# Moving the low parts of U's blocks from VectorE to GpSimd in a decoder layer with expert retrieval

## The chip, the cores and the metric

The kernel runs on one core of one Trainium2 chip. The metric is the device time of one execution in microseconds; a kernel's figure is the median of its runs. One further execution was recorded by the hardware profiler, and all rows below are from it.

## What is computed

The layer has two halves. The first mixes tokens (512 tokens of 1024 features, two groups of eight attention heads, one output projection). The second is a retrieval over 16384 experts of one neuron each, and the change lies in it:

```python
def chunk(hc):                                   # 128 tokens
    q = (hc @ w_q).reshape(-1, PEER_HEADS, PEER_KEY_DIM)
    s1 = jnp.einsum('chd,nd->chn', q[..., :half], k1)
    s2 = jnp.einsum('chd,nd->chn', q[..., half:], k2)
    v1, i1 = lax.top_k(s1, PEER_TOPK)            # 16 of 128
    v2, i2 = lax.top_k(s2, PEER_TOPK)
    cand_s = v1[..., :, None] + v2[..., None, :]
    cand_i = i1[..., :, None] * N_KEYS + i2[..., None, :]
    best_s, best_pos = lax.top_k(cand_s, PEER_TOPK)
    expert = jnp.take_along_axis(cand_i, best_pos, axis=-1)
    g = jax.nn.softmax(best_s, axis=-1)
    act = jax.nn.gelu(jnp.einsum('cd,chkd->chk', hc, u[expert]), approximate=False)
    return jnp.einsum('chk,chkd->cd', g * act, v[expert])
```

Each token picks 128 experts (8 heads of 16). `u` and `v` have 16384 rows of 1024 numbers in float32.

## The kernel before

The tokens are four tiles of 128. For tiles 0 to 2 the kernel does not gather: it multiplies their tokens with all 16384 rows of `u`, in 128 blocks of 128 experts, applies GELU, multiplies by a gate matrix that is zero where a token did not pick an expert, and multiplies the result with all rows of `v`. Tile 3 is done by gathering (`gather_ops`, lines 906 to 923): 128 indirect DMAs of rows of `u` and 128 of `v`, issued by GpSimd, each followed by one VectorE instruction.

Products keep float32 accuracy by splitting: an operand becomes a high part (rounded by ScalarE to the matmul's type `fp32r`) and a low part (operand minus high part), and three products are added: high with high, high with low, low with high (`mm3`, lines 146 to 149).

`u_block` (lines 864 to 881) does one block of U. The 512 KB of rows arrive over SyncE's DMA queue in a tile `raw` (line 866, two buffers); ScalarE makes `hi` (line 870), VectorE or GpSimd makes `lo` (line 871; GpSimd for the blocks in `UPOOL`), two buffers each; TensorE does 8 times the three products of `mm3` with the tokens `h2` (lines 873 and 874; lines 147, 148, 149 in the trace); ScalarE evacuates with GELU into `a` (line 877). Load and split are given a higher priority than what stands around them (`UPRI`), so that the scheduler lays them down early.

Blocks 0 to 55 (`NAHEAD` = `NACT` + `NSPILL`) are done ahead of V, beside the making of the gates. Their results stay in SBUF (`NACT` = 40 buffers) but for the first `NSPILL` = 16, which are written to DRAM (line 879) and read back later (line 988). Beside these blocks run, per token tile:

- `route` (lines 703 to 737): scores on TensorE (line 710), then top-k by VectorE's MAX8, MATCH_REPLACE8 and FIND_INDEX8 (lines 717 to 721, 733 to 737); GpSimd casts the indices (line 723).
- `choose` and `spread` (lines 739 to 804): many VectorE instructions on 128x64 to 128x2048 elements, some on ScalarE (line 765).
- per group of 16 tokens, twice, `hot` (lines 806 to 817): three one-hot tiles `oh` by VectorE, in two buffers each; then `gates` (lines 821 to 837): 16 products of 128x128 (line 831), two times, ScalarE's evacuation (line 834), and a store `g_d` (line 837).

The order written out is the loop at lines 938 to 951: token tiles 0, 1, 2, each of eight groups, two U blocks behind each group (`GPAT`), with `route` and `choose` of the coming tile placed by `WHEN`; four blocks stand ahead of it and two behind the first `choose` (`U0`), and line 952 does what is left of the 56. The framework's scheduler turns this into one fixed list of instructions per engine, by priority and by when it reckons operands to be ready; each engine then works off its list in order, waiting at an instruction until its operands are there. Gathers may so be laid ahead of their place in the text.

The second loop (lines 1032 to 1052) runs over V's 128 blocks: `v_load` loads and splits V's rows and the gated `a` (ScalarE and VectorE), `v_mm` does 18 products of 512 columns (line 1004). From block `NSPILL` on, one U block (56 to 127) follows each V block (line 1039). The gathers of tile 3 are dealt out over the blocks by `RATE` (line 1029), with one rate for b < `NSPILL`, one for b < `NK - NACT` and one for the rest. V can start only when all gates are stored, since each of its blocks reads a slice of all of them (line 970).

Of the kernel before, what the change touches and what calls it, by code (L numbers as in the profile page):

```python
# [9 lines left out]
F32 = mybir.dt.float32  # L10
# [11 lines left out]
P = 128  # L22
D = 1024
KC = D // P
# [12 lines left out]
GSCALE = 32768.0  # L37
ND = NT - 1
DT = ND * P
NACT = 40  # L40
NSPILL = 16
NAHEAD = NACT + NSPILL
VB = 2
WHEN = ((0, 2), (3, 5))
# [9 lines left out]
XAT = (0, 1)  # L54
UPRI = 1000
PACE = 1.02
UPOOL = tuple(range(0, 56, 4))
LAST = 4
VRB = 3
ARB = 3  # L60
# [14 lines left out]
def hybrid_layer(ctx: ExitStack, tc, x, pos, wada, wada_n, cols, w_small, w_in_a, w_in_b, wuk, wuv,  # L75
                 w_out, w_pq, keys, ut, un, pv, gfin, cst, out):
    nc = tc.nc

    def opened(stack, name, **kw):
        if "space" not in kw:  # L80
            kw["reuse_waits"] = "tile"
        return stack.enter_context(tc.tile_pool(name=name, bufs=1, **kw))
# [8 lines left out]
    def one(name, tag="tp"):  # L91
        return ps.tile([P, 512], F32, tag=tag, name=name, bufs=BANKS[tag])

    x1_d = [dram.tile([P, D], F32, name=f"x1_d{j}") for j in range(NT)]
    a_d = [dram.tile([P, DT], F32, name=f"a_d{b}") for b in range(NSPILL)]
    g_d = [dram.tile([P, P // 16, NK, 16], F32, name=f"g_d{j}") for j in range(ND)]
# [49 lines left out]
    def mm3(o, ahi, alo, bhi, blo, start, stop, **kw):  # L146
        nc.tensor.matmul(o, ahi, bhi, start=start, stop=False, **kw)  # L147
        nc.tensor.matmul(o, ahi, blo, start=False, stop=False, **kw)  # L148
        nc.tensor.matmul(o, alo, bhi, start=False, stop=stop, **kw)  # L149
# [24 lines left out]
    def row_back(s, pl, tag, bufs):  # L174
        t = pl.tile([P, D], F32, tag=tag, name=f"gate{s}", bufs=bufs)
        nc.sync.dma_start(t, row_d[s].to_broadcast([P, D]))
        return t
# [95 lines left out]
    for half in range(2):  # L273
# [3 lines left out]
        for k in range(KC):  # L277
            a, b = eff[0][:, k:k + 1], mods[0][:, k:k + 1]
# [301 lines left out]
    for step in SEQ_A.split():  # L580
        what, i = step[0], int(step[1])
# [77 lines left out]
    h2 = []  # L659
# [181 lines left out]
    for n in range(2):  # L841
        his, los = wchunks(wo, [w_pq[n]], 512, f"pq{n}", 16, 2)
        for j in range(NT):
            o = one(f"p_q{n}_{j}", "pl")
# [14 lines left out]
    up = opened(ctx, "up", side="right")  # L859
# [3 lines left out]

    def u_block(b, psum):
        with tc.high_priority(offset=UPRI):
            raw = up.tile([P, KC, P], F32, tag="raw", name=f"u{b}", bufs=2)
            nc.sync.dma_start(raw.rearrange("p k e -> p (k e)"), ut[b])
            hi = up.tile([P, KC, P], F32R, tag="hi", name=f"uhi{b}", bufs=2)
            lo = up.tile([P, KC, P], F32R, tag="lo", name=f"ulo{b}", bufs=2)
            nc.scalar.activation(hi, raw, AF.Copy)  # L870
            (nc.gpsimd if b in UPOOL else nc.vector).tensor_tensor(lo, raw, hi.bitcast(F32), op=ALU.subtract)  # L871
        o = psum(f"p_u{b}")[:, :DT]
        for k in range(KC):
            mm3(o, hi[:, k], lo[:, k], h2[0][:, k], h2[1][:, k], k == 0, k == KC - 1)
        spilt = b < NSPILL
        a = up.tile([P, DT], F32, tag="as" if spilt else "a", name=f"a{b}", bufs=2 if spilt else NACT)
        nc.scalar.activation(a, o, AF.Gelu)  # L877
        if spilt:
            nc.sync.dma_start(a_d[b], a)
            a = a_d[b]  # L880
        acts.append(a)
# [3 lines left out]
    def u_ahead(n):  # L885
        for _ in range(n):
            if nu[0] < NAHEAD:
                u_block(nu[0], lambda n: one(n, ("pj", "po", "ix")[nu[0] % 3]))
                nu[0] += 1
# [76 lines left out]
    def v_load(b):  # L966
        if b % 8 == 0:
            gt = vp.tile([P, ND, P // 16, 8, 16], F32, tag="gt", name=f"gt{b}", bufs=2)
            for j in range(ND):
                nc.sync.dma_start(gt[:, j].rearrange("p g i t -> p g (i t)"),  # L970
                                  g_d[j][:, :, b:b + 8, :].rearrange("p g i t -> p g (i t)"))
            gts[0] = gt
        raw = vp.tile([P, D], F32, tag="raw", name=f"v{b}", bufs=VRB)
        nc.sync.dma_start(raw, pv[b * P:(b + 1) * P, :])
        late = b >= NK - LAST + VB
        if late:
            hi = up.tile([P, D], F32R, tag="hi", name=f"vhi{b}", bufs=2)
            lo = up.tile([P, D], F32R, tag="lo", name=f"vlo{b}", bufs=2)
        else:
            hi = vp.tile([P, D], F32R, tag="vhi", name=f"vhi{b}", bufs=VB)  # L980
            lo = vp.tile([P, D], F32R, tag="vlo", name=f"vlo{b}", bufs=VB)
        nc.scalar.activation(hi, raw, AF.Copy)  # L982
        nc.vector.tensor_tensor(lo, raw, hi.bitcast(F32), op=ALU.subtract)  # L983
        w = vp.tile([P, DT], F32, tag="w", name=f"w{b}", bufs=2)
        a = acts[b]
        if b < NSPILL:
            a = vp.tile([P, DT], F32, tag="ar", name=f"ar{b}", bufs=ARB)
            nc.sync.dma_start(a, acts[b])
        nc.vector.tensor_tensor(w.rearrange("p (g t) -> p g t", t=16), a.rearrange("p (g t) -> p g t", t=16),
                                gts[0][:, :, :, b % 8, :].rearrange("p j g t -> p (j g) t"), op=ALU.mult)  # L990
        if late:
            wh, wl = (up.tile([P, DT], F32R, tag="a", name=f"{n_}{b}", bufs=NACT) for n_ in ("wh", "wl"))
        else:
            wh = vp.tile([P, DT], F32R, tag="wh", name=f"wh{b}", bufs=VB)
            wl = vp.tile([P, DT], F32R, tag="wl", name=f"wl{b}", bufs=VB)
        nc.scalar.activation(wh, w, AF.Copy)  # L996
        last[0] = nc.vector.tensor_tensor(wl, w, wh.bitcast(F32), op=ALU.subtract).ins  # L997
        return wh, wl, hi, lo

    def v_mm(b, j, wh, wl, hi, lo, ns=(0, 1)):  # L1000
        js = slice(j * P, (j + 1) * P)
        for i, (l, r) in enumerate(((wh, hi), (wh, lo), (wl, hi))):
            for n in ns:
                nc.tensor.matmul(accs[2 * j + n], l[:, js], r[:, n * 512:(n + 1) * 512], start=b == 0 and i == 0,  # L1004
                                 stop=b == NK - 1 and i == 2)
# [22 lines left out]

    steps = [RATE[0 if b < NSPILL else 1 if b < NK - NACT else 2] for b in range(NK - LAST)]
    due = 0.0  # L1030
    tail = []
    for b in range(NK):
        ops = v_load(b)
        if b < NK - LAST:
            for j in range(ND):
                v_mm(b, j, *ops)
        else:
            tail.append((b, ops))
        if b >= NSPILL and nu[0] < NK:
            u_block(nu[0], two)  # L1040
            nu[0] += 1
        if b == NK - 24:
            gf = up.tile([P, D], F32, tag="raw", name="gf", bufs=2)
            nc.sync.dma_start(gf, gfin.to_broadcast([P, D]))
            gate2 = row_back(5, up, "raw", 2)
        if b < len(steps):
            due += steps[b] * (2 * TOPK - sum(NGP)) * PACE / sum(steps)
            while due >= 1.0:
                next(gen, None)
                due -= 1.0  # L1050
# [69 lines left out]
```

## Time and profile before

| | us |
|---|---|
| median of three runs | 1631.01 |
| lowest and highest | 1623.51, 1635.10 |
| the profiled execution, its own time | 1633.63 |
| its span in the trace | 1631.9 |

Rows of the trace give a start or a busy time in microseconds; "idle before" and "waited for" name what ended an engine's idle time. TensorE's matmuls overlap, so a single one is shown longer than the pitch at which they follow each other. A granted clock of 1.00 is the full 2.4 GHz.

### The profile page before, as it was taken

Reading aid. Unit: us, or ns where it says so; the run is one execution under the profiler, and the core shown is the slowest. Engines: PE = TensorE matmul, PEld = TensorE weight load, DVE = VectorE, ACT = ScalarE, POOL = GpSimd, SP = SyncE. Lnnn points to the kernel's source line nnn. Section 1 sums busy time; section 2 is a strip of 40 time slices with the busy share of each in tenths; the row PEclk is TensorE's granted clock in tenths of the full one; section 3 lists DMA queues with packets and bytes.
Section 4 is the critical chain, followed back from the end, with each engine's and each line's share of the span. In section 5 each row is a group of like instructions: output and inputs, shape, how many; then the busy total and the mean of one; then the engine's idle time right before and its main releaser. Section 6 shows DMA issues by size and latency. Waiting matters only on the chain.

```text
span 1631.9 us, 23010 instructions
## 1 busy us (share of the span) xinstructions
PE 1545.5 (95%) x8200; PEld 1347.4 (83%) x8202; DVE 1271.8 (78%) x2639; ACT 693.2 (42%) x1110; POOL 533.8 (33%) x406
## 2 busy tenths in 40 slices
PE   5889999998988998999999999999999999999997
PEld 5657776777788888889888999999999999988886
DVE  6898753565899999894458887878878888868886
ACT  4543434444234674875433333333333333333333
POOL 2343112113011112031005555555455445534420
PEclk7988898799999999999999999999999999999999
DMA  8643002413034655576889999989999899879974
GB/s 336 208 153 117 26 27 78 143 65 119 27 102 139 213 203 172 189 267 229 286 269 320 371 334 339 354 306 356 319 333 355 308 348 347 307 279 320 316 263 155
DMA packets 152899, 383.39 MB, mean 235 GB/s; under 512 B 11712, under 2 KB 66384, under 8 KB 149456
## 3 DMA queue, kind: packets, MB, share of 16 engines
q1 hardware_dynamic: 114912, 246.45, 44.8%
q0 software_dynamic: 36864, 134.23, 21.8%
q8 instruction: 64, 1.05, 0.3%
q10 hardware_dynamic: 1008, 1.24, 0.2%
q14 instruction: 51, 0.42, 0.1%
HBM read 349.36 MB, written 32.51 MB: 234 GB/s over the span
## 4 chain that ended last, share of the span: by engine, by line
PE 51%; DVE 3%; DMA 2%; issue 1%; ACT 1%; SPq 0%; POOL 0%; DVEq 0%; POOLq 0%; ACTq 0%
PE acc L1004 30%; PE p_u L149 7%; PE p_u L148 7%; PE p_u L147 7%; DMA ar<-a_d 1%; DVE gu L911 1%; DMA u<-in_ut_dram 0%; ACT st L834 0%; PE p_g L831 0%; DVE oh L815 0%; DVE vlo L983 0%; DVE ulo L871 0%; DMA x1b<-x_d 0%; DMA v<-in_pv_dram 0%; DVE o L1025 0%
## 5 line engine op out<-in xcount | busy, mean ns | idle before, releaser
L147 PE MATMUL p_u<-h,uhi 128*128 128x384 f32 x1024 | 349.3, 341 | 1.3 <-ACT a L877 1.3
L149 PE MATMUL p_u<-h,ulo 128*128 128x384 f32 x1024 | 348.5, 340 | 0.7 <-DVE ulo L871 0.7
L148 PE MATMUL p_u<-h,uhi 128*128 128x384 f32 x1024 | 348.6, 340 | 0.0
L903 POOL DMA_INDIRECT gu<-in_un_dram,e x128 | 191.6, 1497 | 299.1 <-DVE gu L911 204.1
L870 ACT ACTIVATE uhi<-u 128x1024 fp32r<-128x1024 f32 x128 | 135.7, 1061 | 290.1 <-PE p_u L148 246.2
L903 POOL DMA_INDIRECT gv<-in_pv_dram,e x128 | 190.1, 1485 | 207.5 <-DVE acc L922 158.0
L1004 PE MATMUL acc<-vhi,wh 128*128 128x512 f32 x768 | 237.3, 389 | 1.3 <-ACT wh L996 1.3
L1004 PE MATMUL acc<-vlo,wh 128*128 128x512 f32 x768 | 237.3, 389 | 0.5 <-DVE vlo L983 0.5
L1004 PE MATMUL acc<-vhi,wl 128*128 128x512 f32 x768 | 237.1, 389 | 0.0
L147 PEld LDWEIGHTS p_u<-h,uhi 128*128 128x128 f32 x1024 | 194.6, 190 | 4.6 <-ACT a L877 1.7
L148 PEld LDWEIGHTS p_u<-h,uhi 128*128 128x128 f32 x1024 | 195.1, 191 | 2.9
L149 PEld LDWEIGHTS p_u<-h,ulo 128*128 128x128 f32 x1024 | 195.1, 190 | 1.5 <-DVE ulo L871 1.0
L996 ACT ACTIVATE wh<-w 128x384 fp32r<-128x384 f32 x128 | 67.2, 525 | 301.4 <-issue 181.1
L871 DVE TENSOR_TENSOR ulo<-u,uhi 128x1024 fp32r<-128x1024 f32 x114 | 139.2, 1221 | 49.1 <-ACT uhi L870 33.8
L997 DVE TENSOR_TENSOR wl<-w,wh 128x384 fp32r<-128x384 f32 x128 | 71.5, 558 | 135.9 <-ACT wh L996 135.8
L1004 PEld LDWEIGHTS acc<-vlo,wh 128*128 128x128 f32 x768 | 144.0, 188 | 31.0 <-DVE vlo L983 1.1
L1004 PEld LDWEIGHTS acc<-vhi,wl 128*128 128x128 f32 x768 | 144.1, 188 | 30.0
L911 DVE SCALAR_TENSOR_TENSOR gu<-gu,h2n 128x1024 f32<-128x1024 f32 x128 | 158.8, 1256 | 9.7 <-DMA gu<-in_un_dram,e 9.6
L922 DVE SCALAR_TENSOR_TENSOR acc<-gv,w,acc 128x1024 f32<-128x1024 f32 x127 | 162.6, 1280 | 4.6 <-DMA gv<-in_pv_dram,e 4.5
L1004 PEld LDWEIGHTS acc<-vhi,wh 128*128 128x128 f32 x768 | 143.2, 188 | 26.3 <-ACT wh L996 1.7
L983 DVE TENSOR_TENSOR vlo<-v,vhi 128x1024 fp32r<-128x1024 f32 x128 | 156.2, 1220 | 4.4 <-ACT vhi L982 4.4
L982 ACT ACTIVATE vhi<-v 128x1024 fp32r<-128x1024 f32 x128 | 135.5, 1059 | 10.8 <-PE acc L1004 4.3
(348 smaller groups left out, 2363.4 us busy)
## 6 DMA issues: line engine op xcount, KB each, us to landing
u<-in_ut_dram SPq DMA_DIRECT2D x128, 512.0 KB, 5.0
v<-in_pv_dram SPq DMA_DIRECT2D x128, 512.0 KB, 5.0
g_d<-st SPq DMA_DIRECT2D x24, 1024.0 KB, 4.6
gt<-g_d SPq DMA_DIRECT2D x48, 512.0 KB, 10.1
wada<-in_wada_dram SPq DMA_DIRECT2D x12, 1024.0 KB, 5.0
raw_b<-in_w_in_b_dram SPq DMA_DIRECT2D x12, 512.0 KB, 3.7
x<-in_x_dram SPq DMA_DIRECT2D x8, 512.0 KB, 4.5
raw_o<-in_w_out_dram SPq DMA_DIRECT2D x8, 512.0 KB, 3.6
```

Of the source, the lines that this page charges most:

```text
L147: nc.tensor.matmul(o, ahi, bhi, start=start, stop=False, **kw)
L148: nc.tensor.matmul(o, ahi, blo, start=False, stop=False, **kw)
L149: nc.tensor.matmul(o, alo, bhi, start=False, stop=stop, **kw)
L870: nc.scalar.activation(hi, raw, AF.Copy)
L871: (nc.gpsimd if b in UPOOL else nc.vector).tensor_tensor(lo, raw, hi.bitcast(F32), op=ALU.subtract)
L903: nc.gpsimd.indirect_dma_start(out=t, out_offset=None, in_=src, in_offset=bass.IndirectOffsetOnAxis(ap=e0[:, s:s + 1], axis=0))
L911: nc.vector.scalar_tensor_tensor(t, t, 1.0, h2n, op0=ALU.mult, op1=ALU.mult, accum_out=dot0[:, s:s + 1])
L922: nc.vector.scalar_tensor_tensor(acc0, t, w0[:, s:s + 1], acc0, op0=ALU.mult, op1=ALU.add)
L982: nc.scalar.activation(hi, raw, AF.Copy)
L983: nc.vector.tensor_tensor(lo, raw, hi.bitcast(F32), op=ALU.subtract)
L997: last[0] = nc.vector.tensor_tensor(wl, w, wh.bitcast(F32), op=ALU.subtract).ins
L1004: nc.tensor.matmul(accs[2 * j + n], l[:, js], r[:, n * 512:(n + 1) * 512], start=b == 0 and i == 0, stop=b == NK - 1 and i == 2)
```

## The change

`UPOOL` goes from every fourth block of the 56 ahead (14 blocks) to blocks 2 to 53 (52 blocks): their low parts are made by GpSimd. The products of a block are reordered: first the 16 with the high part, then the 8 with the low part. `raw` gets three buffers (`URB`); the same tag is used by two later tiles, at which the number is changed too. `NSPILL` goes from 16 to 19 and `NACT` from 40 to 37, so 56 blocks stay ahead, and three more of them are written to DRAM and read back.

```diff
-NACT = 40
-NSPILL = 16
+NACT = 37
+NSPILL = 19
 NAHEAD = NACT + NSPILL
...
-UPOOL = tuple(range(0, 56, 4))
+UPOOL = tuple(range(2, 54))
+URB = 3
...
     def u_block(b, psum):
         with tc.high_priority(offset=UPRI):
-            raw = up.tile([P, KC, P], F32, tag="raw", name=f"u{b}", bufs=2)
+            raw = up.tile([P, KC, P], F32, tag="raw", name=f"u{b}", bufs=URB)
             nc.sync.dma_start(raw.rearrange("p k e -> p (k e)"), ut[b])
             hi = up.tile([P, KC, P], F32R, tag="hi", name=f"uhi{b}", bufs=2)
             lo = up.tile([P, KC, P], F32R, tag="lo", name=f"ulo{b}", bufs=2)
...
         o = psum(f"p_u{b}")[:, :DT]
         for k in range(KC):
-            mm3(o, hi[:, k], lo[:, k], h2[0][:, k], h2[1][:, k], k == 0, k == KC - 1)
+            for i in range(2):
+                nc.tensor.matmul(o, hi[:, k], h2[i][:, k], start=k == 0 and i == 0, stop=False)
+        for k in range(KC):
+            nc.tensor.matmul(o, lo[:, k], h2[0][:, k], start=False, stop=k == KC - 1)
...
         if b == NK - 24:
-            gf = up.tile([P, D], F32, tag="raw", name="gf", bufs=2)
+            gf = up.tile([P, D], F32, tag="raw", name="gf", bufs=URB)
             nc.sync.dma_start(gf, gfin.to_broadcast([P, D]))
-            gate2 = row_back(5, up, "raw", 2)
+            gate2 = row_back(5, up, "raw", URB)
```

## Rows read from the trace of the kernel before

**Rows 1.** The page's first part: busy us, share of the span, instructions.

```profile
PE 1545.5 (95%) x8200; PEld 1347.4 (83%) x8202; DVE 1271.8 (78%) x2639; ACT 693.2 (42%) x1110; POOL 533.8 (33%) x406
```

**Rows 2.** Windows over the span: length, then busy us of each engine.

```profile
core 0: us, PE busy (x) PEld busy (x) DVE busy (x) ACT busy (x) POOL busy (x), PEclk, DMA share, GB/s
...
457.00:740.00 283.00, 255.36 (x1787) 242.14 (x1788) 267.93 (x865) 170.37 (x207) 54.60 (x35) 0.95 0.56 191
740.00:790.00 50.00, 46.86 (x351) 45.35 (x350) 19.41 (x25) 28.13 (x35) 4.77 (x2) 1.00 0.65 229
...
870.00:1455.00 585.00, 585.00 (x2972) 535.19 (x2971) 476.04 (x604) 209.81 (x288) 300.99 (x206) 1.00 0.94 338
```

**Rows 3.** TensorE's waits from 457 to 790 us: total, times, longest.

```profile
PE p_g L831 <- DVE oh L815: 14.8, 10, 3.1
PE p_g L831 <- ACT st L834: 5.1, 7, 1.6
...
PE p_u L149 <- DVE ulo L871: 0.7, 1, 0.7
```

**Rows 4.** VectorE's instructions in order of time, 732 to 734 us: start, duration.

```profile
732.19 1.22 DVE L871 TENSOR_TENSOR ulo<-u,uhi 128x1024 fp32r<-128x1024 f32 x1
733.33 0.68 DVE L812 TENSOR_TENSOR oh<-tt,iota 128x1024 f16<-128x1024 f16 x1
```

**Rows 5.** Windows of `ulo` alone (PE, PEld, DVE, POOL); then the four `route` stretches summed.

```profile
457.00:740.00 283.00, 127.87 (x367) 71.75 (x368) 42.62 (x35) 30.60 (x12) 0.95 0.56 191
```

```profile
sum 93.00, PE 49.58 PEld 27.83 DVE 16.98 POOL 11.93; mean PE 12.40 PEld 6.96 DVE 4.24 POOL 2.98
```

**Rows 6.** GpSimd's low parts in order of time: start, duration, idle before.

```profile
458.21 2.35 POOL L871 TENSOR_TENSOR ulo<-u,uhi 128x1024 fp32r<-128x1024 f32 x1 [5.27 <-ACT uhi L870]
...
495.69 2.48 POOL L871 TENSOR_TENSOR ulo<-u,uhi 128x1024 fp32r<-128x1024 f32 x1 [10.05 <-ACT uhi L870]
...
726.75 3.29 POOL L871 TENSOR_TENSOR ulo<-u,uhi 128x1024 fp32r<-128x1024 f32 x1 [19.42 <-ACT uhi L870]
```

**Rows 7.** VectorE's instructions beside GpSimd's low parts, and their like without one.

```profile
459.18 0.28 DVE L719 MAX8 v<-wk 128x8 f32<-128x128 f32 x1
...
495.84 2.43 DVE L761 CAST ch<-pb 128x128 f16<-128x128 f32 x1
...
550.46 0.22 DVE L761 CAST ch<-pb 128x128 f16<-128x128 f32 x1
...
616.17 3.91 DVE L800 TENSOR_TENSOR o<-tt,iota 128x2048 f16<-128x2048 f16 x1 [0.40 <-ACT tt L794]
...
639.11 2.21 DVE L727 TENSOR_TENSOR cd<-v 128x96 f32<-128x96 f32 x1
...
703.57 1.21 DVE L800 TENSOR_TENSOR o<-tt,iota 128x2048 f16<-128x2048 f16 x1
...
726.56 1.22 DVE L911 SCALAR_TENSOR_TENSOR gu<-gu,h2n 128x1024 f32<-128x1024 f32 x1
...
727.70 3.42 DVE L911 SCALAR_TENSOR_TENSOR gu<-gu,h2n 128x1024 f32<-128x1024 f32 x1
```

**Rows 8.** Waits of all engines from 457 to 790 us: total, times, longest.

```profile
ACT uhi L870 <- PE p_u L148: 66.0, 26, 8.8
...
POOL gu L903 <- DVE i L787: 29.0, 1, 29.0
```

**Rows 9.** TensorE's instructions in order of time: a run of 57 products of U.

```profile
628.15 0.34 PE L147 MATMUL p_u<-h,uhi 128*128 128x384 f32 x1
...
638.04 0.33 PE L147 MATMUL p_u<-h,uhi 128*128 128x384 f32 x1
```

**Rows 10.** Windows of `p_u` alone (PE, PEld, ACT): U's products from 707 us on.

```profile
707.00:790.00 83.00, 63.78 (x338) 58.87 (x337) 6.73 (x14) 0.98 0.67 238
```

## The prediction

> **What bounds the kernel now.** I read the page's shares first, then the span cut into stretches, then TensorE's waits in the one stretch that is not full, then the instructions of VectorE and GpSimd side by side. The shares name TensorE (95%) and VectorE (78%) [rows 1], but they are means over unlike stretches. Cut up, the span shows two regimes [rows 2]. From 870 to 1455 us, where the U blocks 56 to 127 run beside V's blocks, TensorE is busy for 585.00 of 585 us at full granted clock. From 457 to 740 us, the stretch of the U blocks ahead and the gates, VectorE is busy for 267.93 of 283 us and TensorE for 255.36, at a mean granted clock of 0.95 of 2.4 GHz; from 740 to 790 us VectorE falls to 19.41 of 50 and TensorE is nearly full again. So only 457 to 740 can give something back. There TensorE lost 283 - 255.4 = 27.6 us idle and about 5% of 283 = 14 us of clock: 42 us is all that any change to this stretch can win, some 45 us with the 3 idle ones of 740 to 790 taken in.
>
> TensorE's own waits say for whom: for the one-hot tiles `oh` of VectorE 14.8 us, for ScalarE's gate evacuations 5.1 us, and for a low part of U only 0.7 us, once [rows 3]. The low parts are never late; they hurt because each takes VectorE's time away from `oh`. A low part advances VectorE by 1.14 us (732.19 to 733.33) [rows 4], and 35 of them lie on VectorE before 740 us [rows 5].
>
> **Low parts to GpSimd.** Before 740 us VectorE keeps two (u0, which comes over from GpSimd, and u1), so 33 leave it: 33 x 1.14 = 37.6 us saved. That is what the change would bring if GpSimd worked beside VectorE for nothing. It does not. Of the 12 low parts that GpSimd makes before 740 us, eight make one VectorE instruction run long. At 495.69 us a low part of 2.48 us starts on GpSimd [rows 6]; the CAST that VectorE starts at 495.84 takes 2.43 us, where its twin at 550.46 takes 0.22. The first and last of the eight and one between stand in [rows 7]: 2.43 against 0.22, 3.91 against 1.21, 3.42 against 1.22, so 2.21, 2.70 and 2.20 us lost; over the eight the mean is 2.2. The four without loss fall where VectorE does MAX8, FIND_INDEX8 and MATCH_REPLACE8 of `route`, as the one at 458.21 does: the MAX8 at 459.18 runs beside it in its usual 0.28 us.
>
> So the price depends on what VectorE does. The stretches full of `route` are 457 to 490, 516 to 536, 563 to 581 and 623 to 645 us, 93 us in all. In them lie 16.98 / 1.22 = 14 low parts of VectorE and 11.93 / 2.39 = 5 of GpSimd [rows 5]; of these five one cost anything: the `cd` at 639.11 took 2.21 us [rows 7], where the other four of that shape take 0.24 each (their group's mean of 0.636 over five leaves that), so 2.0. In the other 190 us, where VectorE multiplies and compares one-hot tiles, lie 35 - 14 = 21 and 12 - 5 = 7, and all seven cost 2.2 us. I price the 33 that move so: 21 in such stretches at 2.2 us = 46.2; 12 in `route` stretches at 2.0 / 5 = 0.4 us = 4.8; together 51 against 37.6 saved, 13.4 us more for VectorE. VectorE is idle for 5% of the stretch, and a block that falls there costs nothing: -2.7. Sum +10.7 us. The bounds: all 33 free gives -37.6; all 33 at 2.7 us gives 89 - 37.6 = +51.5. I take +10.7, since seven of seven and one of five are the nearest rows there are.
>
> The Trainium skill ("SBUF — State Buffer", section "Who interferes with whom") says that VectorE instructions with two SBUF inputs and GpSimd instructions that read SBUF share one read interface, and that whichever starts first holds the other off until it ends. By that, a low part that comes while VectorE works would wait itself, and VectorE would lose nothing: near the -37.6 end. The trace shows the wait, but not the gain: the low part at 726.75 takes 3.29 us because a VectorE instruction had begun at 726.56, and the next VectorE instruction is still held 2.2 us [rows 6, 7].
>
> GpSimd itself has room: 45 low parts of about 2.5 us before 740 are 113 us, with 13 gathers and the small casts under 140 of 283. Queued behind each low part there are the index casts of `route` and the gathers. They in turn can hold a low part: gathers waited at the head of that queue for up to 29.0 us on work of VectorE [rows 8]. Today only 14 of the 56 blocks ahead have their low part in that queue.
>
> **High products first.** The same 24 products a block, at the same pitch: 57 products in 9.89 us (628.15 to 638.04), 0.1735 us each, 4.16 us a block [rows 9]. The low part is now wanted 16 x 0.1735 = 2.8 us after the block starts, in place of 0.35 us; that covers GpSimd's 2.4 us instead of VectorE's 1.2. The high part's buffer comes free after 16 products, not 23: 1.2 us earlier. ScalarE waited 66.0 us for that release in 457 to 790 [rows 8], in order, with gate evacuations queued behind. TensorE's 5.1 us on those evacuations is all that can come of it; I take -2 (0 to -5).
>
> **Third buffer for U's rows.** A row block is held longer while GpSimd works (2.4 us for 1.2), and the third buffer covers that. Before, no wait of TensorE goes back to it in this stretch [rows 3]. I take 0, 0 to -2. Behind 870 us more prefetch changes nothing: TensorE is full.
>
> **Three more blocks spilled.** Three stores of 192 KB in a stretch with the DMA engines busy for 56%, and three reads of 192 KB where V starts. In the second loop 19 blocks run V alone before the first U block, not 16, and 37 after the last, not 40; the products are the same and TensorE is full in both. The gathers are dealt out at 2.91 a block, not 2.88. Cost 0, at most +4 where V starts, if a read comes late.
>
> **Sum.** +10.7 - 2 = about +9 us, all in 457 to 740; 0 elsewhere. The profiled execution took 1633.6 us (span 1631.9), 2.6 over the median of 1631.0. So 1642.6 for such an execution, and 1640 for a median, +0.55%. What is late next: TensorE still waits for `oh`.
>
> **Rivals.** *Faster: GpSimd mostly beside.* If low parts fall mainly into `route` stretches and VectorE's idle time, because the third buffer and the early high release let them start sooner, and half of the 51 us of blocking goes, the stretch moves by 25.5 - 37.6 - 2 = -14: 1617. With none of it left: -37.6 - 2, within the 45 that are there: 1591. For it: the saving is sure, the blocking is not; against it: in the 190 us VectorE has almost no gap, and buffers for two low parts let none run far ahead.
>
> *Slower: the fixed order on TensorE.* Each engine works in an order laid down before the run. With low parts gone from VectorE, the gates may be laid earlier among the U products than VectorE, held by GpSimd, delivers `oh`. TensorE then stands at a gate while U products wait behind it, and these are left for the end. The place: token tile 2's one-hots begin at 703.6 us (the instruction `o` in rows 7), and 338 products, 14.1 blocks, were left from 707 us on [rows 10]. In program order 18 blocks would be left (eight groups of 2, and 2). The difference, 3.9 x 4.16 = 16 us, comes on top of +9: +25, 1656, with more half-speed stretches after the gaps up to 1665. It decides from the point where more than about two further blocks are left there (+17 us, 1648). For it: TensorE waits for `oh` now, with U ready [rows 3]. Gathers at the head of GpSimd's queue would work the same way.
>
> *The change does not do what it says:* if VectorE is held but TensorE has slack for it, the stage moves within 5 us: 1631. I count that with the forecast.
>
> **How the numbers follow.** Forecast (blocking about eats the saving, -0.5% to +1%) 0.40; GpSimd mostly beside 0.31; fixed order or queue slower 0.29. A change of 1%, 16 us, is about what a measurement of this kernel can tell from no change; the runs before lie 12 us apart. The forecast's own range is 1624 to 1649. Leaving one in ten out at either end: down to 1600 (most of the blocking gone), up to 1662 (order lost in full). Faster by over 1%: 0.31, a little of the rival's mass lying inside 1% and a little of the forecast's outside. Within 1%: 0.40. Slower by over 1%: 0.29.
>
> **What would show it.** Right: in the stretch from 457 to the first V product, VectorE still busy for over 90%, with some 28 instructions of 2.2 us too many; TensorE's waits go on naming `oh`; TensorE's low-part wait stays small; 870 to 1455 as full as before. GpSimd's low parts at a mean over 2.5 us show the other side of the lock. Wrong to the fast side: VectorE's busy time there falls by over 20 us and V's first product comes before 780 us. Wrong to the slow side: TensorE waits for low parts of GpSimd, or more than 16 U blocks are left when token tile 2's one-hots begin.

## The result, and the profile after

The changed kernel takes 1651.3 us in the median (1648.8 to 1655.6), the kernel before 1632.3 beside it: a ratio of 1.0128, 95% interval 1.0083 to 1.0174. Slower: inside the outer range of 1600 to 1662 us, but above the 1640 that were forecast and above the forecast's own range (1624 to 1649).

The profiled execution has a span of 1647.0 us, 15.1 more than before. The first product of V starts at 815.1 us where it started at 800.0, and from there to the end both need 831.9: the whole loss lies ahead of V. The page's first part of the changed kernel, to set beside [rows 1]:

```profile
PE 1549.4 (94%) x8200; PEld 1354.2 (82%) x8202; DVE 1269.1 (77%) x2601; ACT 707.2 (43%) x1110; POOL 656.6 (40%) x444
```

Windows of the changed kernel, like those of [rows 2] (length, then busy us of PE, PEld, DVE, ACT, POOL, then clock and DMA):

```profile
457.00:740.00 283.00, 241.16 (x1664) 230.19 (x1665) 257.49 (x806) 162.67 (x193) 144.94 (x65) 0.92 0.53 185
740.00:800.00 60.00, 58.84 (x442) 57.45 (x441) 25.16 (x31) 37.65 (x45) 23.83 (x10) 1.00 0.59 204
870.00:1455.00 585.00, 585.00 (x2954) 532.97 (x2953) 479.16 (x609) 215.94 (x286) 310.23 (x204) 1.00 0.94 337
```

From 457 to 740 us GpSimd works 145 us where it worked 55, and VectorE 257 where it worked 268. Both went as the diff says. But TensorE, which was to gain, is busy 241 us in place of 255, at a mean clock of 0.92 in place of 0.95. Its waits up to V's first product, as in [rows 3]:

```profile
PE p_g L832 <- DVE oh L816: 26.8, 11, 5.3
PE tp_s L793 <- DVE eq L772: 7.5, 1, 7.5
PE p_sc L711 <- DVE iu L721: 4.0, 1, 4.0
PE p_g L832 <- ACT st L835: 3.0, 12, 0.3
```

Again the one-hots, 26.8 us where it was 14.8, and nowhere a low part. A hold is what I call it when a VectorE instruction takes longer because it runs beside one of GpSimd. The holds stand in VectorE's instructions in order of time, as in [rows 7]. First GpSimd's in order of time in the changed kernel, an early low part and a late one, as in [rows 6]:

```profile
496.43 2.34 POOL L872 TENSOR_TENSOR ulo<-u,uhi 128x1024 fp32r<-128x1024 f32 x1 [5.94 <-ACT uhi L871]
...
646.69 2.51 POOL L872 TENSOR_TENSOR ulo<-u,uhi 128x1024 fp32r<-128x1024 f32 x1 [3.72 <-ACT uhi L871]
```

Then what VectorE does beside each of the two:

```profile
496.53 2.78 DVE L770 TENSOR_TENSOR eq<-eq,ix 128x1024 f16<-128x1024 f16 x1
...
646.87 2.48 DVE L756 TENSOR_TENSOR pb<-pb,pu 128x128 f32<-128x128 f32 x1
```

The first takes 0.68 us without a hold, the second 0.28. From the first U product to the one-hots of token tile 2 I summed, over all VectorE instructions that take at least 0.4 us longer than the lower quartile of their like (same line, operation and shape), what they take longer. Changed kernel: 24 instructions, 48.0 us, beside 38 low parts on GpSimd. Before: 7 instructions, 15.7 us, beside 10. Summed on to V's first product it is 32 instructions and 60.5 us, beside 52, and before 8 and 17.9, beside 13. The other side pays too; GpSimd's group, and what it waited for:

```profile
L872 POOL TENSOR_TENSOR ulo<-u,uhi 128x1024 fp32r<-128x1024 f32 x52 | 147.3, 2835 | 157.8 <-PE p_u L878 119.6 <-ACT uhi L871 38.1
```

A low part there lasts 2.84 us in the mean, 2.53 before (35.4 us over 14).

VectorE is nevertheless done early with token tile 1. Its instructions around that point:

```profile
698.59 1.28 DVE L816 TENSOR_TENSOR oh<-o,o 128x1024 f16<-128x1024 f16 x2
710.86 2.62 DVE L801 TENSOR_TENSOR o<-tt,iota 128x2048 f16<-128x2048 f16 x1 [10.98 <-ACT tt L795]
```

It stops at 699.9 us and waits 10.98 for transposes that TensorE has not reached. Before, it began tile 2's one-hots at 703.6 without such a wait. Counted from the first U product (459.6 us, before 462.0), VectorE is ready for tile 2 after 240.3 us, where it took 241.6: with 38 low parts on GpSimd and their holds it comes there no sooner and no later.

### The profile page after: what moved, and what is told of

It is laid out like the page before. It is cut to its first block, busy times and chain, and to the rows that moved or that the text cites. A ratio compares the mean times of both kernels' runs of the same rounds, so it can differ in the third digit from the quotient of the medians.

```text
span 1647.0 us, 23056 instructions
## 1 busy us (share of the span) xinstructions
PE 1549.4 (94%) x8200; PEld 1354.2 (82%) x8202; DVE 1269.1 (77%) x2601; ACT 707.2 (43%) x1110; POOL 656.6 (40%) x444
## 4 chain that ended last, share of the span: by engine, by line
PE 71%; DVE 20%; issue 3%; ACT 3%; DMA 3%; POOL 1%; ACTq 0%; DVEq 0%; POOLq 0%; SPq 0%
PE acc L1008 29%; PE p_u L876 17%; PE p_u L878 8%; PE po L551 2%; PE pl L524 2%; DVE oh L816 2%; PE tp L541 2%; PE p_g L832 1%; PE p_b L148 1%; DVE eq L772 1%; PE p_b L150 1%; PE p_b L149 1%; DVE wada L217 1%; DMA v<-in_pv_dram 1%; DVE iu L722 1%
## 5 line engine op out<-in xcount | busy, mean ns | idle before, releaser
L876 PE MATMUL p_u<-h,uhi 128*128 128x384 f32 x2048 | 388.9, 340 | 0.6 <-ACT a L881 0.6
L876 PEld LDWEIGHTS p_u<-h,uhi 128*128 128x128 f32 x2048 | 363.5, 190 | 6.8 <-ACT a L881 0.9
L907 POOL DMA_INDIRECT gv<-in_pv_dram,e x128 | 200.6, 1567 | 184.8 <-DVE acc L926 144.4
L872 POOL TENSOR_TENSOR ulo<-u,uhi 128x1024 fp32r<-128x1024 f32 x52 | 147.3, 2835 | 157.8 <-PE p_u L878 119.6
L878 PE MATMUL p_u<-h,ulo 128*128 128x384 f32 x1024 | 204.5, 339 | 0.0
L878 PEld LDWEIGHTS p_u<-h,ulo 128*128 128x128 f32 x1024 | 182.2, 191 | 0.2
L915 DVE SCALAR_TENSOR_TENSOR gu<-gu,h2n 128x1024 f32<-128x1024 f32 x128 | 154.6, 1223 | 13.7 <-DMA gu<-in_un_dram,e 13.6
L872 DVE TENSOR_TENSOR ulo<-u,uhi 128x1024 fp32r<-128x1024 f32 x76 | 92.6, 1218 | 20.0 <-PE p_u L878 20.0
L835 ACT ACTIVATE st<-p_g 128x512 f32<-128x512 f32 x96 | 92.0, 1094 | 25.3 <-PE p_g L832 25.1
```

Source lines behind the costliest of these rows:

```text
L835: nc.scalar.activation(st[:, :, ts_].rearrange("p i t -> p t i"), o.rearrange("p (t i) -> p t i", i=NK), AF.Copy, scale=1.0 / GSCALE)
L876: nc.tensor.matmul(o, hi[:, k], h2[i][:, k], start=k == 0 and i == 0, stop=False)
L878: nc.tensor.matmul(o, lo[:, k], h2[0][:, k], start=False, stop=k == KC - 1)
L907: nc.gpsimd.indirect_dma_start(out=t, out_offset=None, in_=src, in_offset=bass.IndirectOffsetOnAxis(ap=e0[:, s:s + 1], axis=0))
L915: nc.vector.scalar_tensor_tensor(t, t, 1.0, h2n, op0=ALU.mult, op1=ALU.mult, accum_out=dot0[:, s:s + 1])
```

## The experiments

All ratios are to the kernel before on the same chip, with their 95% interval. The column on the right counts U products in TensorE's instruction list ahead of the last gate of tile 0 and the first of tile 2.

| variant | median us | ratio | U products |
|---|---|---|---|
| before | 1632.3 | 1 | 640, 991 |
| changed | 1651.3 | 1.0128 (1.0083 to 1.0174) | 518, 949 |
| 14 low parts on GpSimd, other edits kept | 1618.8 | 0.9924 (0.9897 to 0.9952) | 645, 1006 |
| before, 52 on GpSimd | 1659.5 | 1.0171 (1.0118 to 1.0225) | 515, 953 |
| changed, U blocks written earlier | 1665.6 | 1.0207 (1.0174 to 1.0240) | 576, 1045 |
| changed, none on GpSimd | 1603.3 | 0.9835 (0.9802 to 0.9869) | 714, 1098 |
| changed, zeros for low parts | 1602.6 | 0.9800 (0.9757 to 0.9843) | 518, 949 |
| changed, three fills with zeros | 1607.3 | 0.9854 (0.9821 to 0.9888) | 518, 949 |
| before, none on GpSimd | 1620.8 | 0.9907 (0.9873 to 0.9940) | 695, 1082 |
| before, high products first | 1625.6 | 0.9950 (0.9930 to 0.9969) | 645, 1006 |
| before, three buffers, 19 spilled | 1632.2 | 1.0002 (0.9977 to 1.0027) | 640, 991 |
| none on GpSimd, holds added | 1666.2 | 1.0227 (1.0191 to 1.0262) | 714, 1098 |
| none on GpSimd, 20 spilled | 1608.1 | 0.9859 (0.9820 to 0.9899) | 714, 1098 |
| before, high first, none on GpSimd | 1611.8 | 0.9890 (0.9857 to 0.9922) | 716, 1099 |

**Which part costs.** Theory after the first look: the loss comes from the low parts on GpSimd, through the order on TensorE, through the holds, or both. The rival: the other three edits.

```diff
-UPOOL = tuple(range(2, 54))
+UPOOL = tuple(range(0, 56, 4))
```

> The changed kernel with GpSimd's low parts put back to every fourth block (14 of 56); high products first, three row buffers and 19 spilled blocks stay. Both theories of the low parts on GpSimd (order on TensorE, hold of VectorE) expect 1625 to 1635 us, that is the time before or a little less. The rival that the loss of 19 us comes from the other three edits expects 1645 to 1655.

Measured 1618.8: 13 us better than before, better than either had it, so a miss for both. The other way round, `UPOOL = tuple(range(2, 54))` alone in the kernel before:

> The kernel before with GpSimd's low parts on blocks 2 to 53 and nothing else. If the move alone makes the loss: 1645 to 1660 us, and TensorE laid down with about as few U products at token tile 2's first gate (953 against 991 before). The low part is wanted after one product here, not after 16: if that hurts too, up to 1670, with TensorE waiting for low parts. The rival (the other edits make the loss) expects 1632.

Measured 1659.5, at the upper end of what was expected. In the old order of products TensorE does wait for low parts of GpSimd, six times, 7.5 us in all, as the expectation had it; with the high products first it does not. So the low parts' move is the loss, with the new edits (1619 to 1651) and without (1632 to 1660), and the rest of the change is a gain.

**Is it the order on TensorE?** The changed kernel has fewer U products ahead of the gates. Writing four blocks more ahead of the loop puts them back:

```diff
-U0 = (4, 2)
+U0 = (6, 4)
```

> The changed kernel with four more U blocks written ahead of the loop (U0 of 6 and 4 in place of 4 and 2), so that TensorE's list has 576 U products at the end of token tile 0's gates, not 518, and 960 at the end of tile 1's, not 864 (640 and 935 before). Theory of the order: TensorE stands less at gates with U ready, some 60 to 96 products of 0.1735 us, 10 to 17 us, are not left for the end: 1635 to 1643 us. Theory of the hold alone (VectorE is late whatever TensorE does): 1648 to 1655.

A miss on both sides: 1665.6. TensorE's list is as meant, but TensorE stands no less. Its waits, up to V's first product:

```profile
PE p_g L832 <- DVE oh L816: 31.7, 10, 6.5
PE acc L1008 <- ACT wh L1000: 11.0, 1, 11.0
PE p_sc L711 <- DVE tt L797: 8.0, 2, 4.5
```

As I read it, the four blocks went in front of the standing, not into it, and V then started with an 11.0 us wait of its own. VectorE was also later: ready for tile 2 only 255.0 us after the first U product (240.3 in the changed kernel), with 56.7 us of lengthening in place of 48.0. So this run does not test the order alone.

**No low part on GpSimd at all.**

```diff
-UPOOL = tuple(range(2, 54))
+UPOOL = ()
```

> The changed kernel with no low part on GpSimd at all; the other three edits stay. VectorE takes all low parts: against 14 on GpSimd it works 12 x 1.14 = 14 us more before 740 and is held 18 us less. If a hold costs what the rows of before show, the time is within 6 us of the variant with 14: 1622 to 1638. If holds cost little and the work of a low part is the larger price, 1640 to 1650.

Measured 1603.3, 1.65% under the kernel before and past the lower end of what was expected. VectorE does every low part of these blocks. Windows of this variant:

```profile
457.00:740.00 283.00, 271.15 (x1999) 258.36 (x1998) 274.05 (x866) 189.80 (x227) 21.82 (x23) 1.00 0.62 214
```

VectorE is busier than in any kernel above (274 of 283), and TensorE is too (271), with the clock at 1.00. No instruction of VectorE is lengthened up to V. TensorE's list changed with it, though (714 products ahead of tile 0's last gate, 518 in the changed kernel), while VectorE is ready for tile 2 in about the same time, 237.2 us after the first U product. The same step in the kernel before:

> The kernel before with no low part on GpSimd, nothing else. The variant of the changed kernel with none took 1603, with 14 it took 1619: the same step of 16 us from 1632 gives 1613 to 1620. If the step needs the other edits: 1630.

Measured 1620.8, 1 us over the range: taking the 14 low parts back from GpSimd gives 0.9%. TensorE's wait for one-hots from 457 to 790 us, 14.8 before [rows 3]:

```profile
PE p_g L831 <- DVE oh L815: 7.5, 8, 1.7
```

VectorE is ready for tile 2 after 239.9 us (241.6 before) here too: the holds that went (15.7 us) were paid for with low parts. TensorE's list has more products ahead (695 and 1082 in place of 640 and 991). How much of the 0.9% comes from the holds and how much from the list, this run does not separate.

**The hold by itself.** GpSimd fills the low parts with zeros. It still writes the same tiles under the same waits for their buffers, but reads nothing in SBUF and no longer waits for ScalarE's high part:

```diff
-(nc.gpsimd if b in UPOOL else nc.vector).tensor_tensor(lo, raw, hi.bitcast(F32), op=ALU.subtract)
+nc.gpsimd.memset(lo.bitcast(F32), 0.0) if b in UPOOL else nc.vector.tensor_tensor(lo, raw, hi.bitcast(F32), op=ALU.subtract)
```

> The changed kernel in which GpSimd fills the 52 low parts with zeros in place of subtracting, so that it writes SBUF but reads nothing there; the low part of U times the high part of the tokens is left out for these blocks. TensorE's, VectorE's and ScalarE's lists are the same, instruction for instruction, as those of the changed kernel. Theory of the hold: VectorE's 48 us of lengthened instructions before token tile 2 go, TensorE stands less, 1605 to 1625 us. Rival, the order on TensorE alone makes it stand: 1643 to 1655.

Measured 1602.6, below what was expected and 49 us under the changed kernel, with the same lists on TensorE, VectorE and ScalarE. That the low part is there earlier is not the gain, since TensorE never waited for one in the changed kernel; nor is it that zeros are multiplied, since the clock is no higher than with real low parts above (0.99, 1.00). The windows of this variant:

```profile
457.00:740.00 283.00, 270.85 (x1993) 259.43 (x1994) 223.39 (x840) 189.59 (x227) 71.72 (x73) 0.99 0.62 216
```

TensorE's wait for the one-hots in it, from 457 to 740 us:

```profile
PE p_g L832 <- DVE oh L816: 4.8, 7, 1.7
```

And GpSimd's group, of the fills:

```profile
L872 POOL MEMSET ulo<- 128x1024 f32 x52 | 50.1, 963 | 211.6 <-PE p_u L878 211.5
```

A fill takes 0.96 us, a subtraction 2.84, so the shorter work was still a rival. Three fills in a row:

> As the variant with zeros, but three fills in a row for each of the 52 blocks, some 2.9 us of GpSimd (one took 0.96), about as long as the subtraction (2.8); lists of TensorE, VectorE and ScalarE as in the changed kernel; the same part of the product is left out. If GpSimd's reads hold VectorE: as with one fill, 1598 to 1610 us. If the length of GpSimd's work made the loss: 1640 to 1655.

Measured 1607.3. GpSimd is busy longer here than in the changed kernel (162.88 us, 144.94 there), VectorE as in the variant with one fill:

```profile
457.00:740.00 283.00, 268.14 (x1971) 256.59 (x1971) 223.29 (x854) 188.65 (x226) 162.88 (x171) 0.99 0.62 215
```

TensorE's and ScalarE's lists were the changed kernel's; VectorE's differed in the order of eight neighbouring instructions, around one gather's. So it is the reads that cost, not GpSimd's time. The opposite: the variant with none on GpSimd, plus 52 additions on GpSimd whose result nobody reads (shown without the spare tile's declaration; 20 spilled blocks make room for it):

```diff
+if 2 <= b < 54:
+    nc.gpsimd.tensor_tensor(spare, raw, raw, op=ALU.add)
```

> No low part on GpSimd (as in the variant that took 1603), but for blocks 2 to 53 GpSimd adds the row block to itself into a spare tile that nobody reads; 20 spilled blocks make room for it. Lists of TensorE, VectorE and ScalarE as in the variant without the additions (run beside it). What is added is the hold alone, on a list with many U products laid ahead (719 at tile 0's end, against 518 in the changed kernel). Hold at 2.0 us for two thirds of some 44 low parts before V: 55 to 60 us for VectorE. If all of it reaches the end: 1650 to 1665. If products laid ahead cover part of it: 1620 to 1645. No hold: 1603.

> The variant with no low part on GpSimd, 20 spilled blocks in place of 19: 1600 to 1607 us, as with 19.

Measured 1666.2 and 1608.1, each 1 us above the upper end of its range. On identical lists, with many U products laid ahead, the added holds cost 58 us. VectorE's lengthening, summed as above, is 46.4 us up to tile 2's one-hots and 10.5 from there to V, together 56.9: as much as reaches the end. The windows of the variant with holds, then of the one without:

```profile
457.00:740.00 283.00, 241.31 (x1591) 229.93 (x1589) 274.02 (x795) 153.09 (x182) 129.28 (x60) 0.92 0.50 166
```

```profile
457.00:740.00 283.00, 269.12 (x1954) 256.08 (x1955) 273.18 (x882) 185.57 (x223) 17.64 (x21) 0.98 0.60 208
```

TensorE's waits in the same stretch of the variant with holds:

```profile
PE p_g L832 <- DVE oh L816: 28.7, 11, 5.7
PE tp_s L793 <- DVE eq L772: 7.0, 1, 7.0
```

VectorE is as busy as without the holds (274 and 273); 28 us of TensorE's work have gone from the stretch (241 in place of 269).

**The other edits.** Products reordered, alone in the kernel before (`mm3` replaced by the two loops of the diff), and buffers and spilling alone:

> The kernel before with the products of the high part first and nothing else. If this edit makes the 13 us that the three edits together gained at 14 low parts on GpSimd: 1616 to 1623 us. If it is the buffers or the spilling: 1630 to 1635.

> The kernel before with three row buffers and 19 spilled blocks, products in the old order, 14 low parts on GpSimd. Expected, from the prediction: no change, 1629 to 1636 us. The rival (these make the 13 us) expects 1616 to 1623.

Measured 1625.6, between the two times expected, and 1632.2. The order of the products gives 0.5%; buffers and spilling alone give nothing. Together they gave 0.76% (14 on GpSimd); whether the third buffer adds to the reordered products is not settled, also not by the last variant, the reordering with none on GpSimd and the old buffers:

> The kernel before with the high products first and no low part on GpSimd; two row buffers and 16 spilled blocks as before. If the third buffer gives something only together with the other two: 1608 to 1615 us. If not: 1600 to 1607, and two lines of the change are all that is worth keeping.

Measured 1611.8. That is in the range expected if the third buffer adds something, but with an interval (0.9857 to 0.9922) that meets those of both variants with three buffers (0.9802 to 0.9869, 0.9820 to 0.9899).

The version to keep is the change with `UPOOL = ()`: 1603.3 us, faster than both kernels.

## Why the prediction held, and where its steps failed

**The stretch** was right: all of it happened between 457 us and V's first product, and 870 to 1455 us is as full as before.

**The hold** was right in kind and a little dear in size. Priced: 51 us for 33 low parts more, 1.55 each. Measured up to tile 2's one-hots: 48.0 - 15.7 = 32.3 us for 28 more, 1.15 each; up to V 60.5 - 17.9 = 42.6 us for 39 more, 1.09 each. Removing the reads removed all but 3.8 us of the lengthening, and 49 us of time.

**The failed step is to take the sum for VectorE as the time of the stretch, with "33 x 1.14 = 37.6 us saved" set off in full against the holds.** The sum for VectorE came out even better than I had it: 29 low parts fewer are 33 us, 32 us of hold more, so about nothing, and VectorE was ready for tile 2 after 240.3 us, not 241.6. The time still rose, because an even sum on VectorE is not an even sum at the end.

The saving was worth little there. Free of holds, the kernel takes 1603 us when VectorE does all these low parts and 1603 when it does almost none (zeros), though VectorE is then ready for tile 2 after 193.6 us, not 237.2. TensorE's work is the end of that stage then: busy for 271 of 283 us, at clock 0.99 to 1.00, on two different lists. Beside holds the saving counted for some: the variant with holds added and all low parts on VectorE takes 1666 us, the changed kernel, with about the same lengthening (56.9 and 60.5 us) and 52 x 1.14 = 59 us less work on VectorE, 1651: 15 us, on another list. The holds were worth most or all of their size: 49 us for 56.7 (60.5 - 3.8) in one pair of identical lists, 58 us for 56.9 in the other. I read "VectorE busy for 268 of 283 us" as the bound; with none on GpSimd VectorE is busy for 267 and the kernel runs 12 us faster, and with the other edits for 274 and 29 us faster.

What the lists show of the reason: VectorE takes the same time to tile 2 in the kernel before, the changed one and the two with none on GpSimd (237 to 242 us), but with low parts on VectorE, more U products are laid ahead of the gates (714 at tile 0's end with none on GpSimd, 640 with 14, 518 with 52). The order is laid down with VectorE's own work reckoned in, and the holds are not in it: TensorE's list is the same with the subtraction as with the fill. So the changed kernel has a list laid for a VectorE that is freed of low parts, and runs it with a VectorE that is held as long as it was freed. That the scheduler's reckoning knows nothing of holds is my inference from these equal lists.

**The rival of the fixed order** described the place well: tile 2's first gate had 949 products ahead of it, not 991, so 7.3 us more were left, and V began 15.1 us late. The sign that I had set for it came, too: 427 products, 17.8 blocks, were left when tile 2's one-hots began at 710.9 us, over the 16 blocks named. (Before it was 375, at 703.6. My 338 were counted from 707 us and only to 790; the last product of these blocks starts at 793.4.) As a cause by itself it falls: on the same list without holds nothing is lost. As a part of the cause it stands, since at an equal pace of VectorE up to tile 2 the kernel with 714 products ahead takes 1603 us and the one with 518 takes 1651. Whether a list with many products ahead would save the changed kernel's 52 low parts on GpSimd is open; the run with four blocks written earlier did not help, but is no clean test of it.

**High products first** was the other mis-sized term: -2 us priced, -8 measured alone and -13 with the third buffer and 14 low parts on GpSimd. I had priced only ScalarE's evacuations, and TensorE's wait for those did not shrink (7.3 us, 5.1 before); the wait for one-hots did (11.0 from 14.8). The reordering also laid 15 more U products ahead of tile 2's first gate (1006 against 991), with TensorE's clock at 0.98 from 457 to 740 in place of 0.95, in an execution of 1620.1 us, one of the faster ones. Which of these makes the 8 us is not shown.

**Buffers and spilling**: priced 0, measured 1.0002.

So the sum was +10.7 - 2, and the parts measured are about +32 (1618.8 to 1651.3) and -13: two errors of opposite sign, partly cancelled. The outer range held, by luck in part: the forecast's own range did not, the value forecast was 11 us too low, and the side that it fell on had a chance of 0.29, given for the fixed order or the queue, neither of which makes the loss alone.

## What to carry to other kernels

Before work is moved from VectorE to GpSimd, look in the trace at what VectorE's instructions do beside GpSimd's: one that takes 2.5 us where its like takes 0.3 is a hold, and it should be charged in full, while the work saved on VectorE is worth only what the engine that sets the end can use. Look also at what the move does to the order of the other engines' lists. Here taking all low parts back onto the busiest helper engine was the gain. A test that separates the two is cheap: let GpSimd write without reading, on otherwise equal lists.

## What the runs showed of the hardware that I had not expected

That GpSimd instructions that only write SBUF hardly hold VectorE, however long GpSimd works: 162.88 us of GpSimd work, most of it fills in threes, beside a VectorE busy time of 223.29, against 223.39 with a third of the fills. The Trainium skill says as much of one kind ("SBUF — State Buffer", section "Who interferes with whom": two-input VectorE instructions contend with GpSimd instructions that read SBUF, not with those that only write), and the runs agree: beside the 52 single fills no two-input TENSOR_TENSOR is lengthened but two that stand behind a held instruction. Four instructions with one input, two TENSOR_SCALAR and two CAST, are held by a fill all the same, until it ends. One fill, and the instruction that it holds:

```profile
611.49 1.04 POOL L872 MEMSET ulo<- 128x1024 f32 x1 [7.25 <-PE p_u L878]
```

```profile
611.56 1.05 DVE L748 TENSOR_SCALAR pa<-t 128x128 f32<-128x128 uint32 x1
```

Without a fill beside it that instruction takes 0.21 us. All the lengthening up to V comes to 3.8 us there, where it was 60.5 with the subtractions.

And that holds pass to the end with little or nothing lost: 58 us of time for 56.9 of lengthening, and 49 for 56.7.
